# Global heads' results for w_oa read through the tiles of outputs and kept gates, and another split of the modulation steps

## The chip, the cores and the metric

The kernel runs on one core of a Trainium2 chip. The metric is the time of one execution in device microseconds (us). The kernel before took 2490.32 us, the median of three runs (2483.99 to 2491.87). All durations from the trace come from one profiled execution of the same kernel.

## The reference

One encoder block over 512 tokens of width 2048. Two token mixers run side by side, each with 8 heads of 128: a global one and a window one. Their results are gated and merged, and a SwiGLU network follows. Both normalizations are modulated (adaLN) by a vector computed from `c`.

```python
c_act = jax.nn.silu(c)
mod = c_act @ w_ada[l] + b_ada[l]
sh1, sc1, g1, sh2, sc2, g2 = [m[:, None, :] for m in jnp.split(mod, 6, axis=-1)]
h = rms_norm(x, norm1_w[l]) * (1.0 + sc1) + sh1
qa, ka, va, qb, kb, vb, ga, gb = jnp.split(h @ w_in[l], offs, axis=-1)
...
ya = global_gqa(qa, ka, va)                      # 8 global heads
yb = neighbourhood_attention(qb, kb, vb, rpb)    # 8 window heads
merged = jax.nn.sigmoid(ga) * (ya @ w_oa[l]) + jax.nn.sigmoid(gb) * (yb @ w_ob[l])
x = x + g1 * (merged @ w_out[l])
...
x = x + g2 * ((jax.nn.silu(h2 @ w_ffn_gate[l]) * (h2 @ w_ffn_up[l])) @ w_ffn_down[l])
```

`w_oa` and `w_ob` have 1024 x 2048 values each, `w_ada` has 2048 x 12288.

## The kernel before

Every float32 factor is split into a high and a low part (`split`, L165 to L169: ACT copies the high part, DVE subtracts it to get the low part), and each product is three matmuls, high x high, high x low and low x high (`mm3`, L184 to L189).

**Weights.** A *unit* (L191 to L202) is one load of 512 KB by SP's DMA queue into a *raw tile*, 128x1024, from a ring of four; ACT and DVE split it into one of three tiles `whl`, and PE uses it in 24 matmuls. A raw tile is free again when both parts of its split are done, and the next load into it waits for that. SP, like every engine, takes its instructions strictly in their order: a load that waits holds back all loads behind it. `form1` (L248) multiplies a pair of output columns: for `w_oa` (loop at L1107) that is two units for a pair, eight pairs, 16 units.

**Modulation steps.** 12288 columns of `mod` are worked out beside the products. Each step is one 512 KB load `mw` from `w_ada` on POOL's queue (three loads ahead) and one accumulate on DVE (L379). `slot()`, called twice a unit, adds `pace["rate"]` to what is due, and a step is issued when a whole one is due. After 16 steps the accumulator is split (`accl`), summed over its rows by PE in bank T or Y (L398), and copied out by DVE (`ada_o`, L402). `pump()`, called after each unit, also runs one function of the list `later`. `finish()` at the end of `w_oa` issues what is left of the steps.

**What passes through DRAM.** Results of the global heads (numbers 0 to 7) and of the window heads (8 to 15), and the gates' products of both mixers, are computed before they are used, and written to DRAM: `y_d`, `sg_a`, `sg_b`. On the chip they pass through a pool `aside` with two small tiles of 128x512 each for two tags: `"y"` (outputs of heads, written at L1032 as `yo`) and `"go"` (gates, `keep_gate`, L630). The gates are all kept before the window heads start.

**The stretch of the change.** The window heads run in a loop over four pairs (L1061). A pair has Q and K products from `w_in`, then two heads `att_b` (L990): scores into bank S, exponentials on ACT, transposes into bank T, their split `pth`/`ptl`, value products into bank Y, copy to `yo`, write to `y_d`. In the last pair, after its K products are issued, the results of the global heads come back for `w_oa`: `attended2(j)` (L1045) takes a raw tile `yr` for heads 2j and 2j+1, loads both halves, and splits the tile into `ya{j}h` and `ya{j}l`, which stay for all of `w_oa`. Four such calls take all four raw tiles.

In `w_oa` each column pair ends with `gated` (L1096): a gate tile `g` from the pool `io` (three buffers, shared with the row sums' `ada_o`) is loaded from `sg_a` by SP, passed through a sigmoid on ACT for the first gates, and DVE multiplies it by the products into `oa`. In the same time `attended` (L1055) brings back the window heads 8 to 15 through the tag `"y"`, one with each `pump()` from the fourth unit on. Their splits `y0h`/`y0l` to `y7h`/`y7l` are the right-hand sides of `w_ob`, which follows.

The order in which each engine gets its instructions is decided when the kernel is built, by a scheduler that goes by its own model of their durations. Its tiles' dependencies hold, but instructions that are issued in one order in the code can stand in another.

Of the kernel before, what the change touches and what calls it, by code (L numbers as in the profile page):

```python
# [14 lines left out]
F32 = mybir.dt.float32  # L15
# [5 lines left out]
P = 128  # L21
WARM = 12, 14
D = 2048
T = 512
# [88 lines left out]
def encoder_block(ctx: ExitStack, tc, xp, xT, c, ada1_w, ada2_w, b_ada, norm1_w, w_in, q_norm_w, k_norm_w, bias,  # L113
                  w_oa, w_ob, w_out, norm2_w, w_gate, w_up, w_down, final_w, rope, out):
    nc = tc.nc
# [10 lines left out]
    aside = tc.alloc_tile_pool(name="aside", bufs=2, side="right")  # L126
# [8 lines left out]
    def buffer(tag, shape, dt, first, name=None):  # L135

        more = wbufs["more"][tag] if wq else 0
        taken[tag] += 1
        n = taken[tag] % (first + more)
        return (wp if n < first else wq).tile(shape, dt, tag=tag, name=name or tag, bufs=first if n < first else more)  # L140

    def raw_tile(name="raw"):
        return buffer("raw", [P, 1024], F32, wbufs["raw"], name)
# [7 lines left out]
    def bank(tag):  # L151
        return ps.tile([P, 512], F32, tag=tag, name=tag, bufs={"mm": 4, "S": 2, "T": 1, "Y": 1}[tag])
# [12 lines left out]
    def split(hi, lo, src, eng=V, pin=lambda ins: ins):  # L165
        with tc.issue_after(hold[0].ins) if hold else contextlib.nullcontext():
            high = pin(S.activation(hi, src, AF.Copy))  # L167
        with tc.issue_after(hold[1].ins) if hold else contextlib.nullcontext():
            latest[:] = [high, pin(eng.tensor_sub(lo, src, hi))]  # L169
# [36 lines left out]
    later = []  # L206
# [5 lines left out]
    pace = {"rate": 0.0, "due": 0.0}  # L212
# [35 lines left out]
    def form1(ws, c0, g, xs, banks, evac):  # L248

        nk = 8 // g  # L250
        n = len(xs)
        for k0 in range(0, n, nk):
            m = min(nk, n - k0)
            for w, bs in zip(ws, banks):
                hi, lo = wsplit(w, k0, m, c0, g * P)
                for kk in range(m):
                    xh, xl = xs[k0 + kk]
                    for j in range(g):
                        sl = slice(j * P, (j + 1) * P)
                        mm3(bs[j], hi[:, kk, sl], lo[:, kk, sl], xh, xl, k0 + kk == 0, k0 + kk == n - 1, 256)  # L260
                    if kk == m // 2 - 1:
                        slot()
                pump()
        for wi, bs in enumerate(banks):
            for j in range(g):
                evac(wi, j, bs[j])
# [573 lines left out]
    y_d = [dram.tile([P, T], F32, name=f"y{h}") for h in range(16)]  # L840
# [202 lines left out]
    ya = []  # L1043

    def attended2(j):  # L1045
        yr = raw_tile("yr")
        for e in range(2):
            nc.sync.dma_start(yr[:, e * T:(e + 1) * T], y_d[2 * j + e])
        hl = [p_m[0].tile([P, 1024], F32R, tag=f"m{2 * j + e}h", name=f"ya{j}{t}", bufs=1) for e, t in enumerate("hl")]
        split(*hl, yr)  # L1050
        ya.extend(tuple(t[:, e * T:(e + 1) * T] for t in hl) for e in range(2))

    p_m = []

    def attended(hl, h):  # L1055
        yr = aside.tile([P, T], F32, tag="y", name="yr")
        nc.sync.dma_start(yr, y_d[h])
        split(*hl, yr)

    later.extend([lambda: None] * 4 + [lambda: pace.update(rate=0.6)])  # L1060
    for hp in range(4):  # L1061
        hh, h0 = hp // 2, 2 * hp
        qs, ks = [pair(p_b, "q", T + 64, 3) for _ in range(2)], [pair(p_b, "k", T, 3) for _ in range(2)]
        form1([w_in], QB + h0 * HD, 2, hT, [[bank("mm"), bank("mm")]], lambda w, j, b: queries(*qs[j], b))
        form1([w_in], KB + h0 * HD, 2, hT, [[bank("mm"), bank("mm")]], lambda w, j, b: tokens_split(*ks[j], b))
        if hp % 2 == 0:
            v = [pair(p_b, "v", 512, NT) for _ in range(NT)]
            for i in range(0, NT, 2):
                vr = raw_tile("vr")
                nc.sync.dma_start(vr.rearrange("p (i n) -> p i n", i=2), v_d[hh][:, i:i + 2])  # L1070
                for e in range(2):
                    split(*v[i + e], vr[:, e * 512:(e + 1) * 512])
        if hp == 3:
            p_h.release()
            p_m.append(tc.alloc_tile_pool(name="p_m", bufs=1, side="left", reuse_waits="tile"))
            for j in range(4):
                attended2(j)
        for j in range(2):
            att_b(h0 + j, qs[j], ks[j], v, slice((hp % 2 * 2 + j) * HD, (hp % 2 * 2 + j + 1) * HD))
# [16 lines left out]
    def gated(src, dst):  # L1096
        def evac(w, j, b):
            g = io.tile([P, T], F32, tag="io", name="g")
            nc.sync.dma_start(g, src[j])
            if any(src[j] is t for t in sg_a[:12]):  # L1100
                S.activation(g, g, AF.Sigmoid)
            V.tensor_mul(dst(j), g, b)
        return evac

    turn = itertools.cycle(("mm", "mm", "S"))
    later.extend([lambda: None] * 3 + [lambda h=h: attended(yT[h], 8 + h) for h in range(8)])
    for j in range(0, KT, 2):  # L1107
        tag = next(turn)
        form1([w_oa], j * P, 2, ya, [[bank(tag), bank(tag)]], gated(sg_a[j:], lambda e: oa[j // 2][:, e * 512:(e + 1) * 512]))
# [5 lines left out]
    for j in range(0, KT, 2):  # L1115
        o = [p_y.tile([P, T], F32, tag="o", name="o", bufs=4) for _ in range(2)]
        tag = next(turn)
# [528 lines left out]
```

## Time and profile before

| | before |
|---|---|
| median of three runs | 2490.32 us (2483.99 to 2491.87) |
| the profiled execution's own time | 2489.47 us |
| its span | 2487.7 us |
| PE busy | 2440.8 us (98%) |
| DVE busy | 2011.0 us (81%) |
| ACT busy | 1070.8 us (43%) |
| moved by DMA | 461.78 MB, 186 GB/s in the mean |

Busy time is the sum of an engine's instructions; the span runs from the first instruction to the last, and the execution's own time is a little longer. A wait of an engine is idle time, put down to the instruction that released it. The windows of the trace give the busy time of PE, of its weight load, of DVE, ACT and POOL in a stretch of time, then the TensorE clock that was granted there (1.00 is the full one), the busy share of the DMA engines, and GB/s.

### The profile page before, as it was taken

To read this page: it belongs to the slowest core of one execution; us is meant where nothing else is said; L and a number is where in the kernel's file an instruction comes from. 1 tells how busy PE (TensorE), PEld (TensorE's weight loads), DVE (VectorE), ACT (ScalarE), POOL (GpSimd) and SP (SyncE) were. 2 spreads that over 40 slices of the span, in tenths; PEclk is the share of its full clock that TensorE was granted. 3 is DMA by queue.
4 is the path that set the end of the run, shared out by engine and by line. 5 is a ranking of instruction groups with operands and counts; after the bars stand their busy time and mean duration, and the time that the engine had idled before them with its cause. 6 is when DMAs were issued, how large, how long until landed. Compare 5 with 4: busy or idle time off the path is not lost.

```text
span 2487.7 us, 42370 instructions
## 1 busy us (share of the span) xinstructions
PE 2440.8 (98%) x17327; PEld 2284.7 (92%) x17327; DVE 2011.0 (81%) x2702; ACT 1070.8 (43%) x1464; POOL 151.6 (6%) x257
## 2 busy tenths in 40 slices
PE   8999999999999989999999999999999999999998
PEld 7888888999888778888999999999999998999997
DVE  8985878987577668756899899898899885687877
ACT  5223555444334433236744444444444454433333
POOL 0100000000012111021000000000000000000010
PEclk9999999999999999999999999999999999999999
DMA  9865232444677787866454454444544456547563
GB/s 362 307 237 160 69 102 77 145 121 143 214 241 240 248 294 248 296 220 218 129 181 146 145 166 149 136 145 144 162 148 158 130 184 217 198 141 241 191 240 129
DMA packets 213731, 461.78 MB, mean 186 GB/s; under 512 B 15152, under 2 KB 59552, under 8 KB 204832
## 3 DMA queue, kind: packets, MB, share of 16 engines
q1 hardware_dynamic: 173872, 308.71, 38.1%
q0 software_dynamic: 30160, 133.77, 15.6%
q10 hardware_dynamic: 9504, 16.58, 1.9%
q8 instruction: 136, 2.23, 0.4%
q14 instruction: 59, 0.48, 0.1%
HBM read 412.84 MB, written 46.17 MB: 185 GB/s over the span
## 4 chain that ended last, share of the span: by engine, by line
PE 71%; DVE 14%; DMA 7%; issue 6%; ACT 2%; POOL 0%; SPq 0%; ACTq 0%; DVEq 0%; POOLq 0%
PE mm L189 14%; PE mm L187 14%; PE mm L188 14%; PE S L187 6%; PE S L189 6%; PE S L188 6%; DVE whl L169 3%; DMA raw<-in_w_down 3%; DVE raw L516 3%; PE Y L187 3%; PE Y L188 3%; PE Y L189 3%; PE T L874 1%; DVE g_acc L623 1%; DMA g<-sga 1%
## 5 line engine op out<-in xcount | busy, mean ns | idle before, releaser
L167 ACT ACTIVATE whl<-raw 128x1024 fp32r<-128x1024 f32 (+1 forms) x483 | 454.1, 942 | 657.8 <-PE mm L189 286.4
L169 DVE TENSOR_TENSOR whl<-raw,whl 128x1024 fp32r<-128x1024 f32 (+1 forms) x483 | 519.5, 1088 | 126.5 <-ACT whl L167 126.1
L167 ACT ACTIVATE whl<-ta 128x1024 fp32r<-128x1024 f32 x124 | 131.2, 1058 | 179.2 <-PE mm L189 110.8
L167 ACT ACTIVATE whl<-tb 128x1024 fp32r<-128x1024 f32 x124 | 131.3, 1059 | 175.5 <-PE S L189 113.0
L169 DVE TENSOR_TENSOR whl<-ta,whl 128x1024 fp32r<-128x1024 f32 x124 | 151.4, 1221 | 46.3 <-ACT whl L167 45.8
L379 DVE SCALAR_TENSOR_TENSOR acc<-mw,cact,acc 128x1024 f32<-128x1024 f32 x124 | 159.3, 1286 | 25.8 <-DMA mw<-in_ada_w 22.0
L169 DVE TENSOR_TENSOR whl<-tb,whl 128x1024 fp32r<-128x1024 f32 x124 | 151.1, 1219 | 6.6 <-ACT whl L167 6.1
L357 POOL DMA_DIRECT2D mw<-in_ada_w x115 | 61.4, 534 | 1406.6 <-DVE acc L379 834.0
L687 DVE TENSOR_TENSOR ta<-raw,ta 128x512 f32<-128x512 f32 x124 | 85.4, 688 | 61.7 <-DMA raw<-in_w_down 26.3
L686 DVE TENSOR_TENSOR ta<-raw 128x512 f32<-128x512 f32 x124 | 85.4, 689 | 39.1 <-DMA raw<-in_w_down 36.7
L187 PE MATMUL mm<-x56h,whl 128*128 128x256 f32 x336 | 92.5, 275 | 0.1
L188 PE MATMUL mm<-x56l,whl 128*128 128x256 f32 x336 | 92.4, 275 | 0.0
L189 PE MATMUL mm<-x56h,whl 128*128 128x256 f32 x336 | 92.4, 275 | 0.0
L188 PE MATMUL mm<-whl,s 128*128 128x256 f32 x320 | 88.3, 276 | 0.6 <-DVE whl L169 0.6
L187 PE MATMUL mm<-whl,s 128*128 128x256 f32 x320 | 88.2, 276 | 0.0
L189 PE MATMUL mm<-whl,s 128*128 128x256 f32 x320 | 88.0, 275 | 0.0
L187 PE MATMUL mm<-x3h,whl 128*128 128x256 f32 x320 | 88.0, 275 | 0.0
L188 PE MATMUL mm<-x3l,whl 128*128 128x256 f32 x320 | 88.0, 275 | 0.0
L189 PE MATMUL mm<-x3h,whl 128*128 128x256 f32 x320 | 88.0, 275 | 0.0
L187 PE MATMUL S<-x56h,whl 128*128 128x256 f32 x320 | 88.0, 275 | 0.0
L188 PE MATMUL S<-x56l,whl 128*128 128x256 f32 x320 | 88.0, 275 | 0.0
L189 PE MATMUL S<-x56h,whl 128*128 128x256 f32 x320 | 88.0, 275 | 0.0
(1879 smaller groups left out, 8922.5 us busy)
## 6 DMA issues: line engine op xcount, KB each, us to landing
raw<-in_w_in SPq DMA_DIRECT2D x133, 512.0 KB, 4.4
mw<-in_ada_w POOLq DMA_DIRECT2D x115, 512.0 KB, 4.7
raw<-in_w_gate SPq DMA_DIRECT2D x92, 512.0 KB, 4.6
raw<-in_w_up SPq DMA_DIRECT2D x88, 512.0 KB, 4.5
raw<-in_w_down SPq DMA_DIRECT2D x88, 512.0 KB, 4.9
raw<-in_ada_w POOLq DMA_DIRECT2D x29, 1024.0 KB, 5.8
raw<-in_w_out SPq DMA_DIRECT2D x48, 512.0 KB, 4.8
ffd<-c SPq DMA_DIRECT2D x10, 1024.0 KB, 4.8
```

The source lines that it names most:

```text
L167: high = pin(S.activation(hi, src, AF.Copy))
L169: latest[:] = [high, pin(eng.tensor_sub(lo, src, hi))]
L187: nc.tensor.matmul(o, lh, rh, start=start, stop=False, **kw)
L188: nc.tensor.matmul(o, lh, rl, start=False, stop=False, **kw)
L189: nc.tensor.matmul(o, ll, rh, start=False, stop=stop, **kw)
L357: mod["queue"].dma_start(w, ada2_w[n * P:(n + 1) * P, :])
L379: behind(V.scalar_tensor_tensor(acc, part, cact[:, k:k + 1], acc, op0=ALU.mult, op1=ALU.add))
L516: V.scalar_tensor_tensor(raw, raw, 1.0, call, op0=ALU.mult, op1=ALU.mult, accum_out=y)
L623: V.tensor_add(acc, acc, b)
L686: V.tensor_sub(t1, b12, b11)
L687: V.tensor_sub(t2_, b22, t1)
L874: nc.tensor.transpose(tp[:, k * P:(k + 1) * P], e[:, k * P:(k + 1) * P], ident)
```

## The change

Heads 0 to 3 still come back through two raw tiles. Heads 4 and 5 now come through the two tiles `"y"` and heads 6 and 7 through the two tiles `"go"`, each head by itself: a load of 128x512 and a split of that size. The rate of modulation steps is 0.68 instead of 0.6 a slot in the window heads, and 0.45 instead of 0.6 in `w_oa`.

```diff
     def attended2(j):
-        yr = raw_tile("yr")
-        for e in range(2):
-            nc.sync.dma_start(yr[:, e * T:(e + 1) * T], y_d[2 * j + e])
         hl = [p_m[0].tile([P, 1024], F32R, tag=f"m{2 * j + e}h", name=f"ya{j}{t}", bufs=1) for e, t in enumerate("hl")]
-        split(*hl, yr)
         ya.extend(tuple(t[:, e * T:(e + 1) * T] for t in hl) for e in range(2))
+        if j < 2:
+            yr = raw_tile("yr")
+            for e in range(2):
+                nc.sync.dma_start(yr[:, e * T:(e + 1) * T], y_d[2 * j + e])
+            split(*hl, yr)
+        else:
+            for e in range(2):
+                yr = aside.tile([P, T], F32, tag="y" if j == 2 else "go", name="yr")
+                nc.sync.dma_start(yr, y_d[2 * j + e])
+                split(*ya[2 * j + e], yr)
...
-    later.extend([lambda: None] * 4 + [lambda: pace.update(rate=0.6)])
+    later.extend([lambda: None] * 4 + [lambda: pace.update(rate=0.68)])
     for hp in range(4):
...
     later.extend([lambda: None] * 3 + [lambda h=h: attended(yT[h], 8 + h) for h in range(8)])
+    pace["rate"] = 0.45
     for j in range(0, KT, 2):
```

The steps between the start of the window heads and the end of `w_oa` are 68 in both kernels: 40 in the heads and 28 in `w_oa` before, 44 and 24 now.

SP's loads, from the last units of the last pair's K products on. Names `y_2434` to `y_2441` are the stored results of global heads 0 to 7 in order, `sga_249` and on those of the kept gates. Before:

```order
L194 DMA raw<-in_w_in 128x4x256 x8
L1048 DMA yr<-y_2434 128x512
L1048 DMA yr<-y_2435 128x512
L1048 DMA yr<-y_2436 128x512
L1048 DMA yr<-y_2437 128x512
L1048 DMA yr<-y_2438 128x512
L1048 DMA yr<-y_2439 128x512
L1048 DMA yr<-y_2440 128x512
L1048 DMA yr<-y_2441 128x512
L194 DMA raw<-in_w_oa 128x4x256 x9
L1099 DMA g<-sga_249 128x512
```

Now, from the same place:

```order
L194 DMA raw<-in_w_in 128x4x256 x8
L1056 DMA yr<-y_2438 128x512
L1051 DMA yr<-y_2434 128x512
L1051 DMA yr<-y_2435 128x512
L1056 DMA yr<-y_2439 128x512
L1051 DMA yr<-y_2436 128x512
L1051 DMA yr<-y_2437 128x512
L194 DMA raw<-in_w_oa 128x4x256 x2
L1105 DMA g<-sga_249 128x512
L1105 DMA g<-sga_250 128x512
L194 DMA raw<-in_w_oa 128x4x256 x5
L1105 DMA g<-sga_251 128x512
```

Heads 6 and 7 are gone from this place: they stand much earlier, among the loads of the last gates' products, since their tiles are free from there on. Two units of `w_oa` now stand directly behind the heads' loads, and the loads of the first three gates, which stood behind nine units, stand behind two and seven.

ACT, from the exponentials of the second half of the last pair's first head (`e`, line L1013) on; `pth` is the high part of the transposed probabilities, `yo` the copy of a head's result, `g` a gate. Before, up to the first gate:

```order
L1013 ACTIVATE e_8123,sm2_8119<-sb_8116,mx2_8118 128x256 x2
L167 ACTIVATE pth_8080<-T_8102 128x512
L167 ACTIVATE pth_8080<-T_8129 128x512
L167 ACTIVATE whl_8352<-raw_8350 128x1024
L1031 ACTIVATE yo_8074<-Y_8061 128x320
L1031 ACTIVATE yo_8074<-Y_8061 128x192
L167 ACTIVATE whl_8388<-raw_8386 128x1024
L1032 DMA y14_2448<-yo_8074 128x512
L1101 ACT_TABLE_LOAD
L1101 ACTIVATE g_8256<-g_8256 128x512
```

Now the stretch with the third and fourth gate:

```order
L167 ACTIVATE pth_8026<-T_8048 128x512
L167 ACTIVATE whl_8381<-raw_8379 128x1024
L1013 ACTIVATE e_8123,sm2_8119<-sb_8116,mx2_8118 128x256 x2
L1107 ACT_TABLE_LOAD
L1107 ACTIVATE g_8369<-g_8369 128x512
L167 ACTIVATE pth_8026<-T_8078 128x512
L1013 ACT_TABLE_LOAD
L1013 ACTIVATE e_8150,sm2_8146<-sb_8143,mx2_8145 128x256 x2
L1107 ACT_TABLE_LOAD
L1107 ACTIVATE g_8373<-g_8373 128x512
L1031 ACTIVATE yo_8101<-Y_8088 128x320
```

Sigmoids of the first gates, which all stood behind the last softmax, now stand between its steps, each with a switch of ACT's function table where the function changes, and one of them stands ahead of a split `pth`.

DVE, in `w_oa`, from the split of the third window head (`y2l`) to the split of the ninth unit. `whl_8480` is the low part of the eighth unit (unit 7, counted from 0), `whl_8533` that of the ninth (unit 8), `oa2` the gated product of the third column pair. Before:

```order
L169 TENSOR_TENSOR y2l_8165<-yr_8424,y2h_8164 128x512
L379 SCALAR_TENSOR_TENSOR acc_8403<-mw_8338,cact_103,acc_8403 128x1024
L169 TENSOR_TENSOR accl_8471<-acc_7750,acch_8470 128x512
L169 TENSOR_TENSOR whl_8480<-raw_8478,whl_8480 128x1024
L1102 TENSOR_TENSOR oa2_8178<-g_8428,S_8348 128x512
L1102 TENSOR_TENSOR oa2_8178<-g_8432,S_8349 128x512
L169 TENSOR_TENSOR y3l_8167<-yr_8474,y3h_8166 128x512
L379 SCALAR_TENSOR_TENSOR acc_8403<-mw_8384,cact_103,acc_8403 128x1024
L169 TENSOR_TENSOR y4l_8169<-yr_8514,y4h_8168 128x512
L379 SCALAR_TENSOR_TENSOR acc_8403<-mw_8407,cact_103,acc_8403 128x1024
L169 TENSOR_TENSOR whl_8533<-raw_8531,whl_8533 128x1024
```

Now, from the same split to the same unit (`whl_8554`); unit 7's split stands ahead of these rows:

```order
L169 TENSOR_TENSOR y2l_8192<-yr_8450,y2h_8191 128x512
L1108 TENSOR_TENSOR oa2_8205<-g_8454,S_8377 128x512
L1108 TENSOR_TENSOR oa2_8205<-g_8458,S_8378 128x512
L379 SCALAR_TENSOR_TENSOR acc_8274<-mw_8327,cact_103,acc_8274 128x1024
L169 TENSOR_TENSOR accl_8359<-acc_7621,acch_8358 128x512
L169 TENSOR_TENSOR y3l_8194<-yr_8499,y3h_8193 128x512
L379 SCALAR_TENSOR_TENSOR acc_8274<-mw_8367,cact_103,acc_8274 128x1024
L363 TENSOR_TENSOR s2_110<-ada_c_8408,vec_102 128x4
L364 TENSOR_TENSOR t2_111<-ada_c_8408,vec_102 128x4
L169 TENSOR_TENSOR y4l_8196<-yr_8538,y4h_8195 128x512
L365 SCALAR_TENSOR_TENSOR s2_110<-s2_110,vec_102 128x4
L169 TENSOR_TENSOR whl_8554<-raw_8552,whl_8554 128x1024
```

Unit 7's split moved from behind the third window head's to ahead of it; unit 8's stays behind the fifth's. From `w_ob` on the orders of the engines are practically those of before.

## The prediction

> **What bounds the kernel now.** I read the page first: span and busy time of each engine.
>
> ```profile
> span 2487.7 us, 42370 instructions
> ...
> PE 2440.8 (98%) x17327; PEld 2284.7 (92%) x17327; DVE 2011.0 (81%) x2702; ACT 1070.8 (43%) x1464; POOL 151.6 (6%) x257
> ```
>
> TensorE is the bound; a change that takes no product away gains only where PE stands still, or runs slowly after it stood still. The change touches the stretch from the last projection to the end of w_oa (821 to 937 us). The waits of PE from 780 to 960 us (who waited for whom, total, times, longest):
>
> ```profile
> PE mm L189 <- DVE whl L169: 5.3, 2, 3.1
> PE mm L187 <- ACT whl L167: 4.9, 1, 4.9
> PE T L398 <- DVE accl L169: 3.0, 1, 3.0
> PE Y L187 <- DVE ada_o L402: 1.6, 1, 1.6
> ```
>
> Then the windows of the stretches where PE waits, and of those behind them (length, busy time and instructions of PE, weight load, DVE, ACT and POOL, granted clock, DMA share, GB/s):
>
> ```profile
> 780.00:800.00 20.00, 17.93 (x96) 15.36 (x96) 16.34 (x18) 6.65 (x14) 5.00 (x9) 1.00 0.66 217
> ...
> 825.00:830.00 5.00, 0.06 (x1) 0.07 (x1) 4.84 (x8) 2.22 (x4) 0.00 (x0) 0.82 0.69 214
> 830.00:835.00 5.00, 5.00 (x17) 4.30 (x18) 4.71 (x9) 4.04 (x10) 0.00 (x0) 0.50 0.92 308
> ...
> 860.00:875.80 15.80, 15.80 (x74) 13.56 (x72) 8.57 (x11) 5.53 (x8) 2.89 (x6) 1.00 1.00 365
> 875.80:879.10 3.30, 0.17 (x2) 0.10 (x1) 3.30 (x5) 1.04 (x3) 0.54 (x1) 1.00 0.71 236
> 879.10:882.60 3.50, 3.50 (x9) 2.81 (x10) 3.44 (x5) 2.38 (x4) 1.68 (x4) 0.54 0.64 127
> ...
> 886.10:888.40 2.30, 0.10 (x2) 0.07 (x1) 2.30 (x5) 0.96 (x2) 0.53 (x1) 1.00 1.04 417
> 888.40:893.00 4.60, 4.60 (x14) 3.75 (x15) 3.47 (x6) 2.40 (x4) 0.00 (x0) 0.63 1.02 377
> ...
> 906.00:909.20 3.20, 0.19 (x2) 0.11 (x1) 3.20 (x6) 0.00 (x0) 0.54 (x1) 1.00 0.87 219
> 909.20:913.40 4.20, 4.20 (x12) 3.41 (x13) 2.82 (x3) 1.27 (x2) 1.59 (x3) 0.61 0.87 304
> ```
>
> Idle in the four waits from 825 on: 4.94 + 3.13 + 2.20 + 3.01 = 13.3 us. After each the granted clock is half for a while: 5.0 x 0.50 + 3.5 x 0.46 + 4.6 x 0.37 + 4.2 x 0.39 = 2.5 + 1.6 + 1.7 + 1.6 = 7.4 us of lost speed. So 20.7 us are to be had here.
>
> **The first wait.** The timeline (start, length, instruction, in brackets the idle time before it and what ended it) has SP's issues and the splits in front of PE; the third row is from the list of SP's own waits:
>
> ```profile
> 788.43 22.25 SPq L1048 DMA_DIRECT2D yr<-y  x8
> 825.11 23.99 SPq L194 DMA_DIRECT2D raw<-in_w_oa  x9
> ...
> SPq L194 <- DVE ya0l L169: 14.3, 1, 14.3
> ...
> 806.32 1.22 DVE L169 TENSOR_TENSOR whl<-raw,whl 128x1024 fp32r<-128x1024 f32 x1
> ...
> 808.65 1.22 DVE L169 TENSOR_TENSOR whl<-raw,whl 128x1024 fp32r<-128x1024 f32 x1
> ...
> 821.02 1.25 ACT L167 ACTIVATE kh<-mm 128x512 fp32r<-128x512 f32 x2 [9.31 <-PE mm L189]
> ...
> 823.86 1.22 DVE L169 TENSOR_TENSOR ya0l<-yr,ya0h 128x1024 fp32r<-128x1024 f32 x1
> ...
> 828.83 1.06 ACT L167 ACTIVATE whl<-raw 128x1024 fp32r<-128x1024 f32 x1 [2.78 <-DMA raw<-in_w_oa]
> ```
>
> The heads' results fill all four raw tiles, so the first unit of w_oa is asked for only when ya0l is split (825.08). Now two raw tiles stay free: they empty with the splits that end at 807.5 and 809.9, and SP issues w_oa's first two units there. They land, and are split, before K's products end (kh at 821.02). PE then waits only for ya0l, in the new order behind 12 score products that end near 823.8 (0.8 us after kh for kl, then 0.11 each) and the first of w_oa's: 1.1 us to 825.08. That is less than the 1.6 us wait above, in a window (780 to 800) of clock 1.00. Two units are 10 us of products; the third is asked for at 825.1, as the first was here, which had landed by 828.8. Term: **-4.94 - 2.5 + 1.1 = -6.3**. The loads of heads 4 and 5 now wait in SP for the writes of y12 and y13, issued at the latest as in the first row; the other rows are the chain's, for a later write and read:
>
> ```profile
> 799.00 0.33 ACTq L1032 DMA_DIRECT2D y<-yo  x1
> ...
> 852.96 7.20 DMA y<-yo
> ...
> 860.22 7.93 DMA yr<-y
> ```
>
> Even a write of 7.20 us lets SP go at 806.2, before the raw tiles are empty: 0. Heads 6 and 7 are asked for far earlier, where the order places them among the loads of the gates' products, with the kept gates long computed: 0.
>
> **The wait that is added.** ACT now has the sigmoids of gates 0 to 3 between the exponentials of the last two heads. Gate 2 takes gate 0's buffer, so SP asks for it when DVE has read gate 0 (oa0), and behind its sigmoid in ACT stands the split pth that PE needs for the value products. Two windows, two pieces of the chain, and the time to landing of all loads of g:
>
> ```profile
> 820.00:840.00 20.00, 14.47 (x68) 12.08 (x67) 17.41 (x30) 13.33 (x24) 0.00 (x0) 0.83 0.49 159
> 835.00:860.00 25.00, 24.87 (x131) 21.30 (x130) 19.45 (x30) 11.88 (x25) 4.78 (x9) 1.00 0.69 233
> ...
> 835.93 0.22 PE mm L188
> ...
> 837.88 0.44 PE T L1021 x4
> ...
> DMA to landing us min/median/max: 2.6/5.6/8.2
> ```
>
> DVE has 27 instructions from ya1l to oa0, 0.58 us each by the first row: 825.1 + 15.7 = 840.8 at most, 839.9 if I add each at its own duration. PE by then: 64 products x 0.214 (15.80 us for 74 in the window from 860) = 13.7, 12 scores and 8 transposes at 0.11, 3 value products: at its wait at 841.5. Gate loads landed in 2.6 to 8.2 us (last row); SP stands at this one load, and the rest of the traffic is one modulation step's, so I take 3.0, near the least. With 0.63 for the sigmoid (a row below) and as much for pth: 844.2 to 845.1. Idle 2.7 to 3.6, I take 3.3, and the 1.7 of clock that such a wait cost above. Behind the waiting sigmoid stand only pth and the exponentials of the last softmax. Term: **+5.0**; bounds +2.3 (839.9, 2.6 to land, no clock lost) and +10.5 (840.8, 8.2 to land).
>
> *Clock.* The 2.20 us wait ending at 888.4 was followed by clock 0.63. The Trainium skill, "TensorE: Matmul & The Clock Gate", section "HAM oscillation — how this bites in real kernels", says "no PE-idle gaps >~3.4µs"; by that rule this wait would cost no clock and the sum below would be 1.7 lower. The trace disagrees, so the trace's price stands.
>
> *Tables.* ACT switches between exp and sigmoid once here before, five times after.
>
> ```profile
> 853.90 1.28 ACT L1101 ACT_TABLE_LOAD   x1
> 855.19 0.63 ACT L1101 ACTIVATE g<-g 128x512 f32<-128x512 f32 x1
> ```
>
> The sigmoid starts as the switch ends: 1.28 us and nothing more. Four more are 5.1 us, in a stretch where ACT was busy 11.88 of 25 us. Two of them come between the value products of the two heads, where ACT has some 5 us of work in all, as long as PE's until it asks for the next pth: 0. The Trainium skill, "ScalarE: Activation LUTs", section "What ACT_TABLE_LOAD costs", puts a switch at about 2.66 us with a drain; by it those two would add an estimated 2.8 us to PE's wait. These rows show no drain.
>
> **The chain of the window heads.** y8 to y15 pass through two buffers, so y10 is asked for when y8 is split, y12 after y10. Weight splits stand in line behind them; PE's first product of unit 4, then DVE and ACT from the timeline:
>
> ```profile
> 859.74 0.38 PE L187 MATMUL S<-ya0h,whl 128*128 128x512 f32 x1
> ...
> 881.85 0.68 DVE L169 TENSOR_TENSOR y4l<-yr,y4h 128x512 fp32r<-128x512 f32 x1
> 885.86 1.28 DVE L379 SCALAR_TENSOR_TENSOR acc<-mw,cact,acc 128x1024 f32<-128x1024 f32 x1 [3.32 <-DMA mw<-in_ada_w]
> ...
> 890.82 0.69 DVE L169 TENSOR_TENSOR y5l<-yr,y5h 128x512 fp32r<-128x512 f32 x1
> ...
> 897.00 0.64 ACT L167 ACTIVATE y7h<-yr 128x512 fp32r<-128x512 f32 x1 [0.28 <-DMA yr<-y]
> ```
>
> Before, unit 7 stood behind y2l and the sum's accl, unit 8 behind y4l and an accumulate whose load was late. After, unit 7 stands behind y0l, 8 behind y4l, 9 behind y5l, and 10 behind y7h on ACT. The chain starts with y14's write: about 850 instead of 852.96, and SP asks for y8 at about 855 instead of 860.22. PE starts unit 4 at 859.74 - 4.94 - 2.5 + 1.1 + 5.0 = 858.4, unit 8 at 879.5, unit 9 at 884.7. With the old steps y4l ends 22.3 after y8: 877.4, no wait. y5l ends 31.3 after: 886.3, split 887.5, wait 2.4. y7h ends 37.4 after: 892.4, split 893.5, wait 1.2. With 0.5 at the row sum and one clock loss of 1.7 that is 5.8 against 8.34 + 4.9 = 13.2 now: term **-7.4**. Four fewer steps lie in w_oa (24 against 28: 2 MB, 5.7 us at the 365 GB/s of the window with DMA share 1.00), so the chain can also be quicker: bounds -13.2 to 0.
>
> **The heads.** Four more steps there, 44 against 40, 5.1 us of DVE; the fullest window has 32.98 of 40 busy with PE at 39.68:
>
> ```profile
> 740.00:780.00 40.00, 39.68 (x198) 34.21 (x197) 32.98 (x50) 17.41 (x36) 6.96 (x13) 1.00 0.80 273
> ```
>
> They hide under products; if not, 1.28 each, 5.1. The 1.6 us wait on ada_o (bank Y) goes, since that copy now comes a whole projection before the next value products; what is late there next is nothing I find: **-1.6**, bounds -1.6 to 0. The halved splits are 4 x 0.6 against 2 x 1.05 on ACT, 0.
>
> **Sum:** -6.3 + 5.0 - 7.4 - 1.6 = -10.3. The profiled execution took 2489.47 (span 2487.7 and 1.8 around it): 2479.2; the median of the runs, 2490.32, lies 0.85 above it, so 2480.
>
> **Rivals.**
> 1. *The chain gives it back* (0.22): y8 is not asked for earlier, the units behind y4l, y5l and y7h wait as long as before. For it: y14's write gains only 3 us. Sum without the third term -2.9: 2487.
> 2. *The chain runs ahead* (0.14): light traffic, y8 at 853, no wait and no clock lost after the gates': -6.3 + 2.3 - 13.2 - 1.6 = -18.8: 2471.
> 3. *Slower* (0.07): an accumulate before a softmax step of heads 2 to 5 waits for its load. Against it: PE hardly waits there now. Price: 3.32 us (the 885.86 row) and 1.7 of clock, 5.0; it decides once PE has under 3 us queued. With five such waits -10.3 + 25 = +15: 2505.
> 4. *It does not do what it says* (0.04): SP stands at y12's or y13's write past 825 and the first wait stays: -10.3 + 6.3 = -4.0: 2486.
>
> **How the numbers follow.** The forecast has 0.53, and most of it lies beyond 0.3% (7.5 us, about what a measurement of this kernel can tell from no change). Faster: 0.46 of it and the 0.14; same: 0.07 of it, 0.22 and 0.04; slower 0.07. So 0.60, 0.33, 0.07. Bounds: -18.8, 2471, and -6.3 + 10.5 = +4.2, 2494; I take one more below for the scatter of the median, cut the upper end to 2490, past rivals 1 and 4, and leave rival 3 out.
>
> **What would show it.** First raw<-in_w_oa before 812 and no PE gap over 2 us at 825; a PE gap of 2 to 4 us near 842 ended by ACT pth, with a gate load before it; no gap at unit 7 and at most 3 us at units 9 and 10; w_oa's last product about 9 us sooner. A PE gap over 5 us near 842, or clock windows below 0.7 in the heads, would make the forecast wrong.

## The result and the profile after

The changed kernel takes 2474.48 us, the median of six runs (2471.66 to 2480.13); the kernel before, on the same chip, 2489.74 us (2483.99 to 2492.89). The ratio is 0.9948, with a 95% interval of 0.9935 to 0.9961: 15.3 us gained of 2490, where 10 were forecast. The profiled execution took 2471.66 us. The page after, its line of the span and that of the engines:

```profile
span 2469.5 us, 42360 instructions
...
PE 2434.0 (99%) x17327; PEld 2279.5 (92%) x17327; DVE 2011.8 (81%) x2704; ACT 1076.2 (44%) x1470; POOL 152.1 (6%) x257
```

The span is 18.2 us shorter in a single execution of each. To see how much of this is the change, take the **stretch** between two marks that the change doesn't touch: PE's first value product of the global heads, and its first product of w_ob. The timeline of PE before, then after (start, length, instruction):

```profile
308.45 0.38 PE L187 MATMUL Y<-pth,st 128*128 128x256 f32 x1
...
937.02 0.38 PE L187 MATMUL S<-y0h,whl 128*128 128x512 f32 x1
```

```profile
309.20 0.38 PE L187 MATMUL Y<-pth,st 128*128 128x256 f32 x1
...
923.92 0.38 PE L187 MATMUL S<-y0h,whl 128*128 128x512 f32 x1
```

628.57 against 614.72: **13.85 us** of the 18.2 come from here. The rest lies after w_oa, mostly in two short waits near 2249 us, with a stretch of half clock behind them. Only the profile of before has this; the thirteen others have shorter waits there or none, and no half clock. Below, the stretch is what is compared from run to run, beside the times.

Who PE waited for from 780 to 940 us, after (total, times, longest), to hold against the same view of before:

```profile
PE T L398 <- ACT acch L167: 2.2, 1, 2.2
PE T L398 <- DVE accl L169: 1.8, 1, 1.8
PE S L187 <- ACT kh L167: 1.0, 1, 1.0
PE S L188 <- DVE kl L169: 0.9, 1, 0.9
PE Y L187 <- ACT pth L167: 0.4, 1, 0.4
PE Y L188 <- DVE ptl L169: 0.4, 1, 0.4
```

All four waits of before are gone: on w_oa's first unit (4.9), on two later units (5.3), on accl (3.0), on ada_o (1.6). What is left stands in other places: the two parts of the last K, and a row sum, the one behind the seventh unit of w_oa (before, the sum that waited stood behind the eleventh). In the stretch the granted clock was half in two pieces of 3.41 us (five before). SP's loads after show the first units asked for at 806.8, not 825.1 us:

```profile
796.67 0.80 SPq L1051 DMA_DIRECT2D yr<-y  x2
806.83 4.24 SPq L194 DMA_DIRECT2D raw<-in_w_oa  x2
...
835.40 0.34 SPq L1105 DMA_DIRECT2D g<-sga  x1
...
841.13 0.34 SPq L1105 DMA_DIRECT2D g<-sga  x1
...
853.40 0.50 SPq L1063 DMA_DIRECT2D yr<-y  x1
...
863.34 0.32 SPq L1063 DMA_DIRECT2D yr<-y  x1
```

### The profile page after: what moved, and what is told of

Read it like the earlier page. It is cut to its first block, busy times and chain, and to the rows that moved or that the text cites. A ratio compares the mean times of both kernels' runs of the same rounds, so it can differ in the third digit from the quotient of the medians.

```text
span 2469.5 us, 42360 instructions
## 1 busy us (share of the span) xinstructions
PE 2434.0 (99%) x17327; PEld 2279.5 (92%) x17327; DVE 2011.8 (81%) x2704; ACT 1076.2 (44%) x1470; POOL 152.1 (6%) x257
## 4 chain that ended last, share of the span: by engine, by line
PE 80%; DVE 11%; DMA 3%; issue 3%; ACT 1%; POOL 0%; DVEq 0%; SPq 0%; POOLq 0%; ACTq 0%
PE mm L189 16%; PE mm L187 16%; PE mm L188 16%; PE S L187 6%; PE S L189 6%; PE S L188 6%; PE Y L187 3%; PE Y L188 3%; PE Y L189 3%; DVE raw L516 2%; DVE whl L169 2%; DMA mw<-in_ada_w 2%; DMA raw<-in_w_down 1%; PE T L189 1%; PE T L188 1%
```

## The experiments

All times are medians; ratios are against the kernel before on the same chip (its median was 2488.2 to 2489.7 us), with 95% intervals. The stretch is that of the one profiled execution, which need not lie near the median; "half" counts the pieces of 3.41 us at half clock in it.

| kernel | time, us | ratio | stretch, us | half |
|---|---|---|---|---|
| before | 2489.74 | 1 | 628.6 | 5 |
| changed | 2474.48 | 0.9948 [0.9935, 0.9961] | 614.7 | 2 |
| changed, again | 2472.41 | 0.9932 [0.9919, 0.9945] | 614.1 | 2 |
| tiles only | 2481.77 | 0.9959 [0.9946, 0.9972] | 619.0 | 2 |
| pace only | 2485.25 | 0.9984 [0.9975, 0.9993] | 626.0 | 5 |
| all sigmoids late | 2471.01 | 0.9922 [0.9907, 0.9937] | 614.3 | 2 |
| sigmoids after K | 2472.62 | 0.9938 [0.9921, 0.9954] | 614.0 | 2 |
| four tiles | 2474.40 | 0.9930 [0.9916, 0.9944] | 612.9 | 1 |
| sums later | 2473.82 | 0.9944 [0.9928, 0.9959] | 615.0 | 2 |
| four tiles, sums later | 2472.34 | 0.9937 [0.9920, 0.9955] | 613.3 | 1 |
| those two, sigmoids after K | 2472.37 | 0.9937 [0.9921, 0.9953] | 610.5 | 0 |
| gate 2 in gate 0's buffer | 2474.15 | 0.9945 [0.9933, 0.9957] | 616.0 | 3 |
| rates 0.76 and 0.3 | 2480.80 | 0.9966 [0.9953, 0.9979] | 620.6 | 3 |
| those rates, four tiles, sigmoids after K | 2469.84 | 0.9925 [0.9913, 0.9937] | 611.5 | 1 |

The same kernel twice differs by 2 us in time and 0.6 in the stretch: differences of that size say nothing.

**The two halves of the change apart.** Tiles only, the old rates:

```diff
-    later.extend([lambda: None] * 4 + [lambda: pace.update(rate=0.68)])
+    later.extend([lambda: None] * 4 + [lambda: pace.update(rate=0.6)])
...
-    pace["rate"] = 0.45
```

> The tiles of the change with the old rates, 0.6 in the heads and in w_oa. The order keeps the gates' sigmoids behind the last softmax, and the splits of units 8, 9 and 10 of w_oa behind y4l, y5l and y6l. Theory A (two parts: the tiles take away the first wait, the pace decides what is left in w_oa): no wait over 0.5 us of PE between 820 and 830 us, the 1.6 us wait on ada_o near 792 still there, and waits of 3 to 8 us with lost clock in w_oa; about 2482 us (2479 to 2485), 8 us under the kernel before. Theory B (the tiles do it all, the pace nothing): as the changed kernel, about 2475.

Pace only: the kernel before with 0.68 and 0.45.

```diff
-    later.extend([lambda: None] * 4 + [lambda: pace.update(rate=0.6)])
+    later.extend([lambda: None] * 4 + [lambda: pace.update(rate=0.68)])
...
+    pace["rate"] = 0.45
```

> The new rates, 0.68 and 0.45, with all results still through the raw ring. Theory A: the first wait near 825 stays at 4 to 5 us with its 2.5 to 3.4 of clock, the 1.6 us wait on ada_o goes, waits of w_oa shrink little because the window heads' chain starts as late as before: 2486 us (2483 to 2490). Theory B for the pace (fewer steps in w_oa alone shorten its waits): 8 to 10 us gained, about 2481.

Both times came out at theory A. The waits of PE with the tiles only, from 700 to 940 us:

```profile
PE mm L189 <- DVE whl L169: 8.3, 1, 8.3
PE Y L187 <- DVE ada_o L402: 1.6, 1, 1.6
PE Y L398 <- ACT yo L1031: 1.3, 1, 1.3
```

and with the pace only, from 780 to 945:

```profile
PE T L398 <- ACT acch L167: 7.7, 1, 7.7
PE mm L187 <- ACT whl L167: 5.7, 1, 5.7
```

The tiles take 9.6 us off the stretch, 7.6 of them at the first wait (0.4 us of idle and no half clock are left there). The wait on bank Y stays, and w_oa stands as long as before: 8.3 us, now all for unit 8, with less clock lost behind it (1.8 us against 5.1) and a new wait of 1.3 us at a row sum. DVE shows why (start, length, in brackets the idle time before):

```profile
880.16 0.69 DVE L169 TENSOR_TENSOR y4l<-yr,y4h 128x512 fp32r<-128x512 f32 x1
882.67 1.28 DVE L379 SCALAR_TENSOR_TENSOR acc<-mw,cact,acc 128x1024 f32<-128x1024 f32 x1 [1.83 <-DMA mw<-in_ada_w]
883.87 1.22 DVE L169 TENSOR_TENSOR whl<-raw,whl 128x1024 fp32r<-128x1024 f32 x1
```

The unit's split stands behind a window head and behind an accumulate whose load is late, as in the kernel before; y8 is asked for at 860.27 here, no earlier than before. The pace alone leaves the first wait (5.7) and gives 2.5 us, 1.6 of them at bank Y. On top of the tiles it gives 4.3 (619.0 to 614.7). The pace changes two things at once, how many steps fall into w_oa and where the scheduler puts them; no run separates these.

**The early sigmoids.** With the new pace the order has the sigmoids of gates 0 and 1 on ACT ahead of kh, the high part of the last K, which PE needs next. ACT after:

```profile
812.89 1.06 ACT L167 ACTIVATE whl<-raw 128x1024 fp32r<-128x1024 f32 x1 [6.80 <-DMA raw<-in_w_oa]
818.00 1.28 ACT L1107 ACT_TABLE_LOAD   x1 [4.05 <-DMA g<-sga]
819.29 1.15 ACT L1107 ACTIVATE g<-g 128x512 f32<-128x512 f32 x2
820.35 1.04 ACT L167 ACTIVATE whl<-raw 128x1024 fp32r<-128x1024 f32 x1
821.30 1.06 ACT L167 ACTIVATE kh<-mm 128x512 fp32r<-128x512 f32 x2
```

ACT stood 4.05 us at the load of gate 0, then came the switch of tables, two sigmoids and a split, and kh only behind them: PE waits 1.0 us for it and then 0.9 for kl. Two edits take the sigmoids away from there. All of them behind the last split pth:

```diff
+            last_pt[:] = latest[:1]
...
-                S.activation(g, g, AF.Sigmoid)
+                with tc.issue_after(last_pt[0].ins):
+                    S.activation(g, g, AF.Sigmoid)
```

> The changed kernel, with the sigmoids of all gates issued after the last split pth, so that ACT does not stand at a gate's load ahead of kh. Theory A (the waits of 1.0 and 0.9 us on kh and kl and the half clock from 824 on come from the early sigmoids): no wait over 0.5 us between 820 and 825, no half clock before 860, 3 to 4 us under the changed kernel's 2474.5: 2471. Rival: the time comes back behind it, since gates and row sum now crowd ACT and DVE from 855 to 880: waits there grow from 4 to 7 us or more, 2474 to 2478.

And only behind the split of the last K, which moves two sigmoids and their table switch from ahead of kh to behind ya3h and nothing else on any engine:

```diff
+        last_k[:] = latest[:1]
...
-                S.activation(g, g, AF.Sigmoid)
+                with tc.issue_after(last_k[0].ins):
+                    S.activation(g, g, AF.Sigmoid)
```

> The changed kernel, with the sigmoids of the first gates issued only after the split of the last K: in the order the first two and their table switch move from ahead of kh to behind ya3h, on ACT, and nothing else moves. Theory A (the waits on kh and kl and the half clock from 824 on come from these two instructions standing at a gate's load): from the first value product of the heads to the first product of w_ob 3 to 4 us less than the changed kernel's 614.7 us: 611.2; no half clock before 870; time 2471. Rival (chains that hang on DMA keep their time, so PE only waits later): 614 us, with waits over 6 us at the row sum near 870.

The waits on kh and kl went in both, and the stretch hardly changed: 614.3 and 614.0. With the sigmoids all late, PE waits 2.4 us for a split ptl that stands behind an accumulate waiting for its load, and loses clock behind it. So time came back, but not where the rival put it: the row sum's wait fell, to 2.6 us. The median, 2471.01, is theory A's number. The profiled execution took 2474.99 us, the longest of the four, so its stretch doesn't speak for the median, and what this edit gains stays open. With the exact edit the rival was right: the time comes back at the row sum, though with 5.1 us and not over 6 (waits of PE, sigmoids after K):

```profile
PE T L398 <- ACT acch L167: 3.3, 1, 3.3
PE T L398 <- DVE accl L169: 1.8, 1, 1.8
```

Counted from the stretch's first mark, PE reaches this sum 3.1 us earlier than in the changed kernel, waits 1.1 us longer at it (5.1 against 4.0), and loses 3.1 us of clock behind it against 1.7. That leaves some 0.7 us, which is what the stretch gained. What ends the wait is the load of y10 (y2h on ACT). It is issued at 861.90 in that run and used at 870.00, 8.1 us later; in the changed kernel it is issued at 864.23 and used at 870.88, 6.65 later. From the first mark the load starts 3.5 us earlier and is used 2.0 earlier. The changed kernel's own second execution, which lost no clock behind kh and came to the sum 1.7 us earlier than the first, shows the same: 8.05 us for this load, 5.0 us of waiting and two pieces of half clock. Why the load takes longer when it starts sooner is not shown.

**Window heads through four tiles.**

```diff
-        yr = aside.tile([P, T], F32, tag="y", name="yr")
+        yr = aside.tile([P, T], F32, tag="y" if h % 2 else "go", name="yr")
```

> The changed kernel, with window heads 8, 10, 12 and 14 read back through the tag go, so four tiles in place of two. Theory A (the row sum's waits of 2.2 and 1.8 us at 871 and the half clock after them come from loads of y9 and y10 that stand in SP at the write of y15): y10 is asked for before 858 in place of 864.2, the two waits go with their clock, 5 to 6 us under the changed kernel: 2469. Rival (the row sum waits for ACT and DVE, which are full there, or for the DMA): waits stay at 3 to 4 us, 2474.

The stretch is 1.8 us shorter (1.2 against the second execution of the changed kernel), not 5 to 6. The wait on acch stays at 2.1 us, closer to the rival: y2 is split at 856.70 now, but the order puts acch on ACT behind y6h and a weight split:

```profile
872.46 0.63 ACT L167 ACTIVATE y6h<-yr 128x512 fp32r<-128x512 f32 x1 [1.07 <-DMA yr<-y]
872.99 1.04 ACT L167 ACTIVATE whl<-raw 128x1024 fp32r<-128x1024 f32 x1
873.94 0.61 ACT L167 ACTIVATE acch<-acc 128x512 fp32r<-128x512 f32 x1
```

**Row sums one unit later** (in w_oa), alone, then with the four tiles, then with the sigmoids after K as well:

```diff
-        soon.append((1 if few else 2, lambda: row_products(hl, tag, dst, then)))
+        soon.append((1 if few else 2 + pace["lag"], lambda: row_products(hl, tag, dst, then)))
...
-    pace["rate"] = 0.45
+    pace.update(rate=0.45, lag=1)
```

> The changed kernel, with the row sums' products one unit later while w_oa runs. Theory A (the 4.0 us wait at 871 is only for acch and accl, which stand behind y2's splits in ACT and DVE): the wait and its clock go, 5.7 us, but unit 8, split at 879.0, is then late for PE by some 2 us: 3 to 4 us less in the stretch, 611 us, 2471. Rival (the stretch is set by the window heads' chain or the DMA, whatever PE waits for): unit 8 waits for all of it, 614 us.

> Both of the last two edits on w_oa: window heads through four tiles, and row sums one unit later, with the early sigmoids of the changed kernel kept. Theory A (with the row sum out of the way, the chain of the window heads is what sets unit 8, and four tiles shorten it): unit 8 does not wait, idle of PE from 855 to 900 under 1.5 us, no half clock there, 609.5 us in the stretch, 2469. Rival (loads, not tiles, set it): idle over 3 us, 612 us.

> All three edits together: sigmoids after the last K, window heads through four tiles, row sums one unit later. If the three costs are apart from each other: 8 to 9 us less than the changed kernel in the stretch, 606 us, 2466 us. If they trade against each other: no better than the best of them, 610 us, 2470.

Alone it gives nothing: PE reaches the sum 3.4 us later in the stretch and still waits 4.0 and 0.7 us, since the scheduler put acch behind y4h too. The rival's price came out, though at the sum and not at unit 8. With four tiles 613.3 us, and 3.8 us of idle from 855 to 900: the rival was right. With all three edits 610.5 us and no half clock in the stretch: 4.3 us less than the changed kernel, half of what was expected if the costs were apart, and at the number for costs that trade (610). 3.4 of the 4.3 us are clock, 1.7 of them at the row sum, where the cost hangs on how the waits of one execution fell (last section). The time, 2472.37, doesn't tell it from the changed kernel.

**The added wait that was forecast.** The prediction priced the wait for gate 2 at 5.0 us on the ground that gate 2 takes gate 0's buffer. To build that case:

```diff
-            g = io.tile([P, T], F32, tag="io", name="g")
+            g = first[0] if src[j] is sg_a[2] else io.tile([P, T], F32, tag="io", name="g")
+            first.append(g)
```

> The changed kernel, with gate 2 in the buffer of gate 0 instead of the one that ada_o leaves; all engines keep their order. This is the case that the prediction priced at +5.0. Theory A (the price was right, the buffer was wrong): SP asks for gate 2 when oa0 is read, at about 841 instead of 835.4; PE waits 3 to 4.5 us for pth, with one half clock: 4 to 5 us more than the changed kernel's 614.7 in the stretch from the first value product of the heads to the first product of w_ob, 619, and 2478.5. Rival (the load is short, or the later waits shrink by as much): under 616, 2475.

The case didn't arise. The two gates changed places: SP asks for one at 841.08, when ada_o's buffer is free, and for the other at 845.87, when gate 0 has been read (oa at 845.2). Gate 2, which has gate 0's buffer in this edit, can only be the second. The waits on pth and ptl are those of the changed kernel (0.5 and 0.4 us), and the price of the forecast wait wasn't measured.

**Other rates.** With 0.76 and 0.3 the row sums stand at the third and fourth unit of w_oa. Alone, and with four tiles and the sigmoids after K:

```diff
-    later.extend([lambda: None] * 4 + [lambda: pace.update(rate=0.68)])
+    later.extend([lambda: None] * 4 + [lambda: pace.update(rate=0.76)])
...
-    pace["rate"] = 0.45
+    pace["rate"] = 0.3
```

> The changed kernel with rates 0.76 in the heads and 0.3 in w_oa, so that the two row sums stand at the third and fourth unit of w_oa instead of the sixth and seventh, where the window heads come back. Theory A (the pace acts by where the row sums fall): the 4.0 us wait near 871 and the half clock after it go; unit 8 waits up to 2 us; 611 in the stretch, 2471. Rival (the window heads' chain sets the stretch): the waits come back at the units' splits, 614, 2474.

> As the last one, with the sigmoids after the last K and the window heads through four tiles. If the three costs (early sigmoids, two tiles, place of the row sums) are the ones left in this stretch: idle of PE under 3 us from 820 to 937, no half clock, 608 in the stretch, 2468. Rival (they trade, as sigmoids and row sum did): 611, 2472.

w_oa becomes free of most waits, as expected: from its first product to w_ob's 95.9 and 92.1 us against 99.25. But the heads pay, and neither theory had that for the rates alone. Waits of PE from 700 to 940 us, the rates alone:

```profile
PE S L187 <- ACT kh L167: 4.1, 1, 4.1
PE Y L398 <- ACT vh L167: 2.7, 1, 2.7
PE mm L189 <- DVE whl L169: 2.0, 3, 0.9
```

and with the other two edits:

```profile
PE Y L398 <- DVE ada_o L402: 2.9, 1, 2.9
```

With the rates alone the stretch is 620.6, 6 us longer than the changed kernel's: the early sigmoids wait for their gate's load until 826.96 us, and PE for kh 4.1 us. With the sigmoids after K this is gone, and only a row sum in the heads waits, 2.9 us, for bank Y. The stretch is 611.5 us, the rival's number, and the time 2469.84 us, the lowest median; by ratio the run with all sigmoids late is as low (0.9922 against 0.9925). On the same chip the changed kernel took 2472.41; the intervals of their ratios overlap, so whether one of these is better than the changed kernel isn't settled. All are clearly faster than the kernel before.

## Why the prediction was right, and where it was not

The forecast was 2480 us, from -10.3 us; the time was 2474.48, inside the range, and faster by more than 0.3%. It was 3.5 us off in the stretch, less than its largest error, since two errors of opposite sign partly cancel.

The account below takes idle time of PE and lost clock, which is half of PE's busy time at half clock, as the forecast did. These two explain the differences between the runs: take them off, and 601.2 to 603.4 us of the stretch are left in all fourteen profiles. Before they were 19.3 and 7.7 us, after 10.0 and 3.4. By the forecast's own terms, in the stretch:

*The first wait, -6.3.* Measured: 5.5 us of idle and 2.5 of clock before (0.2, 0.3 and 4.9 us), 1.9 and 1.7 after: -4.4. In the second execution of the changed kernel 1.5 us of idle and no half clock: -6.5. The mechanism held, and the tiles alone show it (-7.6). The 1.1 us that were to remain were put at the wrong place and priced too low: not ya0l but kh and kl are late, by 1.9 us that also cost 1.7 of clock, because two sigmoids stand ahead of them. They do so with the new rates only; with the tiles alone the gates' loads stand behind ten units. The prediction followed the sigmoids of gate 2 and looked at what stands behind them; it didn't do so for gates 0 and 1.

*The added wait, +5.0.* **This is the step that failed.** Gate 0 has been read close to when the forecast had it (at 841.1, forecast 839.9 to 840.8). But measured are 0.4 on pth and 0.4 on ptl, no clock lost: +0.8, below its lower bound of 2.3. "Gate 2 takes gate 0's buffer" was wrong. The third buffer of that pool held ada_o, written out by POOL, and gate 2 takes that one. POOL's issue, then SP's wait from 833 to 837 us:

```profile
833.40 0.80 POOL L403 DMA_DIRECT2D md<-ada_o  x1 [18.80 <-DVE rs L1016]
...
SPq L1105 <- DMA md<-ada_o: 2.9, 1, 2.9
```

This write landed 1.9 us after its issue, at 835.3, and SP asks for gate 2 at 835.40. When ACT comes to its sigmoid, at 841.2, the gate is there. Gate 3 is the one that waits for gate 0's reading (oa at 840.43, asked for at 841.13), and behind its sigmoid stands the copy yo, which has time.

*The window heads' chain, -7.4.* Measured: 8.3 us of idle and 5.1 of clock before, 4.0 and 1.7 after: -7.7 (in the second execution 5.0 and 2.0: -6.4). The sum was right, and so was the chain's start (y8 forecast at 855, asked for at 853.40). The places weren't: units 9 and 10 don't wait at all, the row sum does, for 4.0 us instead of 0.5, behind y2 on ACT and DVE. So the size is partly luck. In the four runs that worked on this sum PE still stands 3.2 to 4.7 us at it and at the units around it, against 4.0 and 5.0 in the two executions of the changed kernel: where one wait shrinks, another takes most of it.

*Bank Y, -1.6.* Measured -1.6: no wait on ada_o is left.

The sum of the measured terms is -4.4 + 0.8 - 7.7 - 1.6 = -12.9 of the 13.85 of the stretch; in the second execution -6.5 + 0.9 - 6.4 - 1.6 = -13.6 of 14.45. The remaining 0.9 us are shorter waits and rounding. Forecast were -10.3: the 3.5 us between are the added wait (4.2 too much), less the first wait (1.9 too good), the chain (0.3) and those 0.9.

*The rivals.* That the chain stands as long as before was true of the tiles alone (8.3 us of idle), and the pace change prevents it. The slower case, an accumulate that waits for its load ahead of a step of the heads, shows in the run with all sigmoids late (2.4 us and one half clock), but not at the rates of the change.

*The two rules.* On the clock the trace's price was right, and the rule of the Trainium skill ("TensorE: Matmul & The Clock Gate", section "HAM oscillation — how this bites in real kernels", no gaps over some 3.4 us) was not: 1.9 us of idle, in two pieces of 1.0 and 0.9, were followed by half clock. On the tables, the switch took 1.28 us in all five places, with the next activation starting right behind it in four of them (818.00 and 819.29 in the rows above; in the fifth it waits for DVE), as the rows of before had it; the drain that the Trainium skill adds ("ScalarE: Activation LUTs", section "What ACT_TABLE_LOAD costs") doesn't show here.

## What to carry to other kernels

Before saying which buffer a tile gets, count every tile of its pool, those of another kind too: here ada_o moved the wait elsewhere. When a kernel has several waits on one chain of loads, expect that one taken away alone comes back in the next place (early sigmoids, later sums); all three together gave 4.3 us of the stretch in one execution, and no clear gain in time. A change of pace also moves what the scheduler places around the steps; here it moved sigmoids, sums and splits, and each had to be looked for on the engine on which it now stands ahead of something. An instruction that moves ahead of another has to be followed for every gate: the forecast did it for gate 2 and missed gates 0 and 1.

## What the runs showed of the hardware

The half clock follows windows on a fixed grid, and half a window of idle is enough. All its pieces in the stretch are whole multiples of 3.41 us and start, within one execution, at multiples of 3.41 us from each other (before: 828.2, 879.4, 889.6, 910.1). The rows below are windows of two neighbouring pieces of that grid: behind the length comes PE's busy time, and behind POOL's the granted clock, 1.00 or 0.50. Changed kernel:

```profile
820.94:824.35 3.41, 1.53 (x11) 1.34 (x12) 2.61 (x4) 3.41 (x6) 0.00 (x0) 1.00 0.16 48
824.35:827.76 3.41, 3.41 (x15) 3.05 (x14) 3.41 (x5) 3.39 (x6) 0.00 (x0) 0.50 0.50 168
```

Gate 2 in gate 0's buffer:

```profile
824.51:827.92 3.41, 1.59 (x7) 0.89 (x6) 1.59 (x2) 3.41 (x6) 0.00 (x0) 1.00 0.05 17
827.92:831.34 3.42, 3.13 (x12) 2.97 (x13) 2.49 (x4) 3.42 (x7) 0.00 (x0) 0.50 0.47 158
```

Four tiles, sums later and sigmoids after K:

```profile
867.59:871.00 3.41, 1.76 (x9) 1.50 (x9) 1.67 (x2) 1.94 (x3) 1.06 (x2) 1.00 1.04 412
871.00:874.42 3.42, 3.42 (x18) 2.97 (x17) 3.14 (x5) 1.37 (x3) 0.53 (x1) 1.00 1.03 411
```

1.53 and 1.59 us busy of 3.41 cost the next window its clock; 1.76 didn't. Over the fourteen profiles, from 700 to 1000 us, 21 such windows at full clock had 1.82 us of idle or more, and all were followed by half clock; 18 had between 0.85 and 1.71, and none was. So a wait of some 2 us costs nothing or 1.7 us of clock, by where it falls on the grid: 1.81 and 0.23 us at one row sum cost it in the run with four tiles and later sums, while 1.80 and 0.23 us did not in the one that has the sigmoids after K as well. Two short waits in one window count as one long one.

A window that is itself at half clock needs less idle to be followed by another. Sigmoids after K, then all sigmoids late:

```profile
873.70:877.11 3.41, 2.71 (x6) 2.16 (x7) 3.41 (x9) 2.38 (x4) 1.06 (x2) 0.50 0.77 255
877.11:880.53 3.42, 3.42 (x9) 2.66 (x8) 3.39 (x5) 1.09 (x2) 0.74 (x2) 0.50 0.93 322
...
877.02:880.44 3.42, 2.83 (x7) 2.29 (x8) 3.42 (x7) 0.63 (x1) 0.53 (x1) 0.50 1.08 394
880.44:883.85 3.41, 3.41 (x18) 2.98 (x17) 2.42 (x4) 2.85 (x4) 1.04 (x2) 1.00 1.06 398
```

In the fourteen profiles, again from 700 to 1000 us, all ten windows at half clock with 0.70 us of idle or more were followed by half clock, and none of those with 0.59 or less.
